# Program order at four output projections, three raw buffers in the first stage, and seven products of quarters in the first squared-ReLU MLP of a two-block fp32 transformer kernel

## Chip, cores and metric

The kernel runs on one core of one Trainium2 chip. The metric is the device time of one execution in microseconds. Three runs of the kernel before gave a median of 1999.02 us (1995.79 to 1999.51).

## What is computed

Two blocks of a transformer work on one sequence of 512 tokens with 1024 features, in fp32. The first block is a mixer (a forgetting attention and a chunked attention beside it), a cross attention to 256 memory rows, and a SwiGLU MLP. The second has an mLSTM layer and an MLA layer, each with an MLP of a squared ReLU behind it, and its norms are modulated by rows that are computed from a vector c. Cut to what this change touches:

```python
def rms_norm(x, g):                                   # over the 1024 features
    return x * lax.rsqrt(jnp.mean(x * x, -1, keepdims=True) + EPS) * g

def sqrelu_mlp(h, w1, w2):                            # w1: 1024x4096, w2: 4096x1024
    return jnp.square(jax.nn.relu(h @ w1)) @ w2

# first block
mix = concat([o_f, o_c]) @ w_out;   x = x + rms_norm(mix, g_mix_post)      # projection 1
ca  = attention_to_memory(...) @ w_mem_o;  x = x + rms_norm(ca, g_mem_post) # projection 2
x = x + rms_norm(swiglu(rms_norm(x, g_ffn_pre)), g_ffn_post)
# second block, for l in 0 (mLSTM), 1 (MLA)
ada = silu(c) @ ada_w[l] + ada_b[l];  sh1, sc1, g1, sh2, sc2, g2 = split(ada, 6)
y = mixer_l(modulate(rmsnorm(x), sh1, sc1)) @ w_out_l                       # projections 3 and 4
x = x + g1 * rmsnorm(y);  h = modulate(rmsnorm(x), sh2, sc2)
x = x + g2 * rmsnorm(sqrelu_mlp(h, w1[l], w2[l]))
```

## The kernel before

**Numbers in two parts.** Every operand of TensorE is kept as a rounded part `hi` and a rest `lo`. `prod` (L447, L448, L449) makes each product by three matmuls, hi·hi, hi·lo and lo·hi, on 128x512 or 128x256 outputs. ACT makes `hi` and DVE makes `lo = x - hi`: for activations in `parts` (L629, L630), for weights in `split` (L307 and L308, or L317 and L318 with a gain). Weights come by 512 KB DMAs on SP's queue into `raw` buffers, of which four may be live (`pump`), and `tick` deals out their splitting in pieces as TensorE's work is written down.

**What sets the order.** The program is written in one pass and a scheduler then orders the instructions of each engine by priority; inside an engine they run in that order, each waiting for what it needs. Work written under `hot` is moved ahead by 300 places. `ordered()` switches the scheduler off for PE, ACT, DVE and Pool within its block, so that they keep the order in which the code is written.

**Boundaries.** `boundary` closes a sublayer and opens the next. For each of the four token tiles t, `y_of(t)` makes the output of the tile (in `out_lin` the second half of its columns, 24 matmuls of 128x512, since the first half of all tiles stands ahead of it), `a(t)` adds the normed output to the stream x (mean of squares at L579, reciprocal root on POOL at L562 and L568, addition at L651), `scaled(t)` scales it for the next sublayer (L598), and `put(t)` transposes it by eight PE transposes (L609), modulates it in the second block (L616 on DVE, L619 on ACT) and splits it (L629, L630). The next sublayer's first products (`first`) need `put` of tiles 0 and 1 first. `out_lin` (L716) is the output projection and calls `boundary` with `fixed=True`: `put(t-2)` then stands four products into `y_of(t)` and `put` of the last tiles between the first units. With `fixed=False` these steps stand after `y_of(t)`. The four calls of `out_lin` are at L1215, L1898, L1920 and L1940; the last two modulate. `mlp` (L1344) also ends in `boundary`, with `fixed=True` for the SwiGLU MLP and the last MLP, which has no sublayer behind it (`nxt` is None), and `fixed=False` for the first squared-ReLU MLP.

**The two squared-ReLU MLPs.** `relu2` computes the 32 column blocks of `h @ w1` in 16 pairs, in five groups (6, 8, 6, 6, 6 blocks), with the down products of a group behind its up products. The first MLP has `h` of class `HT` and takes each pair by `relu_pairs`: 48 matmuls of 128x512. The second has `h` of class `HS`: after the first group (three pairs) each of the other 13 pairs is made by `wino` (L492): seven products of quarters (Strassen's scheme) with 84 matmuls of 128x256 (L510). That takes sums of weight quarters (`split7`, L331), sums of quarters of `h` (`quarters`, L473) and five 128x256 combinations of the results per pair (L524 to L534) on DVE.

**Background rows.** The modulation rows `ada` are computed by DVE from weights that POOL's queue loads (`row_by`: multiply-add at L873, DMA at L878, halves added at L882, then split at L630, one matmul with ones at L891, result read at L908). One step of this generator is written whenever TensorE's written work has passed 1.9 units of cost (`step_bg`). `y2` is the number of empty steps between the split of a half row and its matmul.

**The first stage.** `mixer1_values` starts as soon as x[0] and the first weights are there. `self.before` (L1087) names ahead of which weight load the DMAs of x[1], and of x[2] and x[3], go into SP's queue.

## Time and profile before

| | |
|---|---|
| median of three runs | 1999.02 us (1995.79 to 1999.51) |
| the profiled execution: its time, its span | 1995.13 us, 1993.3 us |
| mean granted clock of TensorE over the span | 0.991 |
| PE busy | 1941.7 us, 97% of the span |
| DVE busy | 1276.1 us, 64% |
| ACT busy | 1037.3 us, 52% |
| POOL busy | 351.5 us, 18% |
| chain of work that ended last, by engine | PE 90%, ACT 4%, DVE 4%, issue 1% |

The page has one execution; its own time lies 1.8 us above its span and 3.9 us under the median. A busy share is an average over stages, so the waits of PE and the windows of single stages say more than the share of an engine over the whole span.

### The profile page before, as it was taken

How to read it: one execution, taken by the hardware profiler on the slowest of the kernel's cores; microseconds unless marked ns; L12 is line 12 of the kernel's file. 1: busy time of each engine (PE TensorE's matmuls, PEld its weight loads, DVE VectorE, ACT ScalarE, POOL GpSimd, SP SyncE). 2: the span in 40 equal slices, each digit the busy share in tenths (PEclk: the TensorE clock that was granted, in tenths of full speed). 3: DMA queues.
4: the chain of work that ended last, by engine and by line, in shares of the span. 5: the costliest groups of instructions: out<-in, count | busy, mean ns of one | idle time of the engine just before them, and what ended most of it. 6: DMA issues, size and time to landing. Idle time of an engine off the chain costs nothing.

```text
span 1993.3 us, 28466 instructions
## 1 busy us (share of the span) xinstructions
PE 1941.7 (97%) x10222; PEld 1645.7 (83%) x10222; DVE 1276.1 (64%) x2517; ACT 1037.3 (52%) x2282; POOL 351.5 (18%) x703
## 2 busy tenths in 40 slices
PE   7999999998999999999998999999999999999998
PEld 5888987878888888878877888888888879989987
DVE  5756655765766785666885557654458655656765
ACT  6767775456334343455646442433566555545443
POOL 1331111211221231212232222210020012000000
PEclk9999999999999999999999999999999999999999
DMA  6332333442655563345462446533042121233222
GB/s 202 91 80 65 117 125 112 145 138 64 190 181 164 175 212 127 103 128 154 125 192 94 126 161 222 165 112 119 29 126 69 64 85 43 75 107 116 96 82 77
DMA packets 175246, 241.95 MB, mean 121 GB/s; under 512 B 20107, under 2 KB 117536, under 8 KB 175104
## 3 DMA queue, kind: packets, MB, share of 16 engines
q1 hardware_dynamic: 150704, 170.53, 27.1%
q0 software_dynamic: 24400, 69.60, 11.4%
q8 instruction: 80, 1.31, 0.3%
q14 instruction: 62, 0.51, 0.1%
HBM read 237.88 MB, written 2.20 MB: 120 GB/s over the span
## 4 chain that ended last, share of the span: by engine, by line
PE 90%; ACT 4%; DVE 4%; issue 1%; DMA 0%; POOL 0%; SPq 0%; DVEq 0%; POOLq 0%; ACTq 0%
PE ps L447 25%; PE ps L448 24%; PE ps L449 24%; PE ps L510 6%; PE ps L1033 1%; PE ps L609 1%; PE ps L1823 1%; ACT s L317 1%; PE ps L1852 1%; PE ps L1004 1%; PE ps L1583 1%; DVE s L318 1%; PE ps L1017 1%; PE ps L1320 1%; ACT junk L579 1%
## 5 line engine op out<-in xcount | busy, mean ns | idle before, releaser
L447 PE MATMUL ps<-s,s 128*128 128x512 f32 (+3 forms) x2468 | 940.2, 383 | 28.5 <-ACT s L629 28.5
L448 PE MATMUL ps<-s,s 128*128 128x512 f32 (+3 forms) x2468 | 928.3, 377 | 0.1
L449 PE MATMUL ps<-s,s 128*128 128x512 f32 (+3 forms) x2468 | 924.4, 377 | 2.0 <-DVE s L630 2.0
L447 PEld LDWEIGHTS ps<-s,s 128*128 128x128 f32 (+1 forms) x2468 | 467.2, 190 | 114.6 <-ACT s L629 31.5
L449 PEld LDWEIGHTS ps<-s,s 128*128 128x128 f32 (+1 forms) x2468 | 466.3, 189 | 91.3 <-DVE s L630 2.5
L448 PEld LDWEIGHTS ps<-s,s 128*128 128x128 f32 (+1 forms) x2468 | 467.3, 189 | 83.7 <-DVE s L630 1.0
L307 ACT ACTIVATE s<-raw 128x512 fp32r<-128x512 f32 x329 | 186.3, 623 | 177.3 <-PE ps L449 130.7
L308 DVE TENSOR_TENSOR s<-raw,s 128x512 fp32r<-128x512 f32 x329 | 213.9, 688 | 87.8 <-ACT s L307 85.9
L873 DVE SCALAR_TENSOR_TENSOR u<-araw,cond,u 128x512 f32<-128x512 f32 x224 | 168.5, 752 | 31.9 <-DMA araw<-in_ada_w 21.9
L317 ACT ACTIVATE s<-raw,cols_all 128x256 fp32r<-128x256 f32 (+1 forms) x305 | 142.7, 544 | 59.5 <-PE ps L449 25.2
L318 DVE SCALAR_TENSOR_TENSOR s<-raw,cols_all,s 128x256 fp32r<-128x256 f32 (+1 forms) x305 | 146.2, 538 | 30.8 <-ACT s L317 30.5
L878 POOL DMA_DIRECT2D araw<-in_ada_w x192 | 104.2, 543 | 283.2 <-DVE u L873 236.2
L630 DVE TENSOR_TENSOR s<-u,s 128x512 fp32r<-128x512 f32 x118 | 80.1, 689 | 115.1 <-ACT s L629 92.6
L510 PEld LDWEIGHTS ps<-s,s 128*128 128x128 f32 x1092 | 130.2, 188 | 1.0
L568 POOL TENSOR_SCALAR sm<-sm,sm 128x1 f32<-128x1 f32 x34 | 16.5, 485 | 647.8 <-ACT junk L579 519.8
L510 PE MATMUL ps<-s,s 128*128 128x256 f32 x1092 | 130.5, 280 | 0.0
L629 ACT ACTIVATE s<-u 128x512 fp32r<-128x512 f32 x118 | 72.2, 627 | 53.6 <-PE ps L449 27.0
L630 DVE TENSOR_TENSOR s<-ps,s 128x512 fp32r<-128x512 f32 (+3 forms) x100 | 59.5, 606 | 36.9 <-ACT s L629 35.8
L1465 ACT ACTIVATE u<-ps 128x512 f32<-128x512 f32 x38 | 22.6, 596 | 114.9 <-PE ps L449 111.0
L1368 DVE TENSOR_TENSOR u<-ps,u 128x512 f32<-128x512 f32 x80 | 54.3, 687 | 39.7 <-PE ps L449 39.6
L629 ACT ACTIVATE s<-ps 128x512 fp32r<-128x512 f32 (+3 forms) x100 | 51.2, 526 | 23.5 <-PE ps L609 10.2
L318 DVE SCALAR_TENSOR_TENSOR s<-raw,cols_mix,s 128x128 fp32r<-128x128 f32 (+2 forms) x152 | 52.4, 401 | 11.0 <-ACT s L317 10.6
(261 smaller groups left out, 2011.0 us busy)
## 6 DMA issues: line engine op xcount, KB each, us to landing
raw<-in_mlp_w SPq DMA_DIRECT2D x128, 512.0 KB, 3.8
araw<-in_ada_w POOLq DMA_DIRECT2D x192, 256.0 KB, 3.4
raw<-in_w_gate_up SPq DMA_DIRECT2D x44, 512.0 KB, 4.5
raw<-in_w_in SPq DMA_DIRECT2D x24, 512.0 KB, 4.1
raw<-in_a_w_in SPq DMA_DIRECT2D x24, 512.0 KB, 4.6
raw<-in_w_down SPq DMA_DIRECT2D x22, 512.0 KB, 3.8
raw<-in_w_mem_kv SPq DMA_DIRECT2D x16, 512.0 KB, 3.5
araw<-in_kv_ada_w POOLq DMA_DIRECT2D x32, 256.0 KB, 3.6
```

What stands on the lines that cost most here:

```text
L307: A.activation(hi[:, sl, cl], src[:, sl, cl], AF.Copy)
L308: f.tensor_tensor(out=lo[:, sl, cl], in0=src[:, sl, cl], in1=hi[:, sl, cl].bitcast(F32), op=ALU.subtract)
L317: A.activation(hi[:, i, :], src[:, i, :], AF.Copy, scale=g)
L318: V.scalar_tensor_tensor(out=lo[:, i, :], in0=src[:, i, :], scalar=g, in1=hi[:, i, :].bitcast(F32), op0=ALU.mult, op1=ALU.subtract)
L447: self.nc.tensor.matmul(ps, lhsT=ah, rhs=bh, start=first and i == 0, stop=False)
L448: self.nc.tensor.matmul(ps, lhsT=ah, rhs=bl, start=False, stop=False)
L449: self.nc.tensor.matmul(ps, lhsT=al, rhs=bh, start=False, stop=last and i == n - 1)
L510: nc.tensor.matmul(ps, lhsT=l[:, k, :], rhs=m[:, k, :], start=first and k == e == 0, stop=k == 3 and e == 2, skip_group_check=True)
L629: self.nc.scalar.activation(hi, x, AF.Copy)
L630: self.nc.vector.tensor_tensor(out=lo, in0=x, in1=hi.bitcast(F32), op=ALU.subtract)
L873: V.scalar_tensor_tensor(out=acc, in0=raws.pop(j), scalar=vec[:, j:j + 1], in1=acc, op0=ALU.mult, op1=ALU.add)
L878: nc.gpsimd.dma_start(out=raws[j], in_=ws[:, j, :])
```

## The change

1. The boundaries of the four output projections run in program order: `boundary(fixed=True)` is written inside `self.ordered()` and without `hot`.
2. All MLP boundaries now have `fixed=False`. That moves the one of the SwiGLU MLP (the last one has nothing behind it, and the first squared-ReLU MLP had it so).
3. In the first stage three `raw` buffers may be live and not four, and the loads of x[1] to x[3] each stand one weight load later in SP's queue.
4. The input of the first squared-ReLU MLP is an `HS` and not an `HT`, so that 13 of its 16 up pairs are made by seven products of quarters.
5. `y2` is 2 and not 1: one more background step lies between the split of a half row and its matmul.

```diff
-... y1=0, y2=1, y3=0, ...
+... y1=0, y2=2, y3=0, ...
@@ __init__
+        self.rcap = BUF["raw"] - 1
@@ pump
-                if self.raw_live + len(loaders) <= BUF["raw"]:
+                if self.raw_live + len(loaders) <= self.rcap:
@@ boundary
-        hot = lambda: self.hot("hb")
-        with nullcontext():
+        hot = nullcontext if fixed else lambda: self.hot("hb")
+        with self.ordered() if fixed else nullcontext():
             for t in range(NT):
@@ mixer1
-        self.before = {1: [lambda: get(1)], 3: [lambda: get(2), lambda: get(3)], 6: [biases]}
+        self.before = {2: [lambda: get(1)], 4: [lambda: get(2), lambda: get(3)], 6: [biases]}
...
             self.mixer1_values(h, vf, w)
+        self.rcap = BUF["raw"]
@@ mlp
-    def mlp(self, blocks, up, w_down, g, nxt, first, ready=None, caps=None, fixed=True):
+    def mlp(self, blocks, up, w_down, g, nxt, first, ready=None, caps=None):
...
-                self.boundary(y_of, nxt, first, fixed=fixed)
+                self.boundary(y_of, nxt, first, fixed=False)
@@ relu2
-        self.mlp(BUF['mb'], up, self.a["mlp_w2_2"][l], g, nxt, first, ready, BUF['mc'], fixed=nxt is None)
+        self.mlp(BUF['mb'], up, self.a["mlp_w2_2"][l], g, nxt, first, ready, BUF['mc'])
@@ the mLSTM layer's projection
-        hn = HT(self, KD)
+        hn = HS(self, KD)
         self.out_lin(a["a_w_out_2"][0], ho, g, nxt(4, 3, hn), self.relu_pairs(hn, a["mlp_w1_2"][0], 0, BUF["fp"], True), "head")
```

Lines of the changed kernel are one higher from L152 on and two higher from L1092 on.

**ACT at projection 1.** `s_802` and `s_804` are the halves of the next sublayer's input that `put(1)` fills, `s_818` to `s_823` weights of the cross attention, `x_10` the stream's token tile 2, `ps_3719` and `ps_3721` the output of tile 3. In the kernel before ACT has:

```order
L579 ACTIVATE junk_3713,sm_3712<-x_10_91 128x1024
L317 ACTIVATE s_818_3726<-raw_3510,cols_all_1926 128x256 x4
L317 ACTIVATE s_819_3735<-raw_3523,cols_all_1926 128x256 x4
L317 ACTIVATE s_822_3758<-raw_3540,cols_all_1926 128x256 x4
L317 ACTIVATE s_823_3767<-raw_3557,cols_all_1926 128x256 x4
L579 ACTIVATE junk_3773,sm_3772<-ps_3719 128x512
L629 ACTIVATE s_802_3677<-ps_3738 128x4x128
L629 ACTIVATE s_804_3681<-ps_3743 128x4x128
```

and in the changed one:

```order
L580 ACTIVATE junk_3715,sm_3714<-x_10_91 128x1024
L318 ACTIVATE s_818_3728<-raw_3510,cols_all_1926 128x256 x2
L630 ACTIVATE s_802_3679<-ps_3740 128x4x128
L630 ACTIVATE s_804_3683<-ps_3745 128x4x128
L318 ACTIVATE s_818_3728<-raw_3510,cols_all_1926 128x256 x2
L580 ACTIVATE junk_3775,sm_3774<-ps_3721 128x512
```

The two halves of `put(1)` stood behind 16 weight pieces and the mean of squares of tile 3, and now stand behind two weight pieces. On PE the transposes of `put(1)` moved with them, from the end of tile 3's 24 matmuls to their middle.

**ACT at projection 3.** `u_2022`, `u_2023` (before) and `u_1998`, `u_1999` (changed) are tile 1 on its way through the modulation, and `s_2015`, `s_2017` and `s_1993`, `s_1994` the halves of the MLP's input. Before:

```order
L307 ACTIVATE s_2031_10540<-raw_10259 128x512 x2
L307 ACTIVATE s_2032_10549<-raw_10266 128x512 x2
L307 ACTIVATE s_2036_10582<-raw_10348 128x512 x2
L307 ACTIVATE s_2037_10591<-raw_10363 128x512 x2
L579 ACTIVATE junk_10597,sm_10596<-ps_10533 128x512
L619 ACTIVATE u_2022_10516<-ps_10554,cols_1324_6645,cols_1385_7069 128x128 x2
L619 ACTIVATE u_2023_10518<-ps_10563,cols_1324_6645,cols_1385_7069 128x128 x2
L598 ACTIVATE u_2042_10601<-x_10_91,sm_10531 128x512
L598 ACTIVATE u_2043_10603<-x_10_91,sm_10531 128x512
L629 ACTIVATE s_2015_10491<-u_2022_10516 128x4x128
```

Changed:

```order
L580 ACTIVATE junk_10469,sm_10468<-x_10_91 128x1024
L308 ACTIVATE s_2007_10482<-raw_10215 128x512 x2
L620 ACTIVATE u_1998_10458<-ps_10496,cols_1330_6756,cols_1405_7233 128x128 x2
L620 ACTIVATE u_1999_10460<-ps_10505,cols_1330_6756,cols_1405_7233 128x128 x2
L630 ACTIVATE s_1993_10435<-u_1998_10458 128x4x128
L630 ACTIVATE s_1994_10438<-u_1999_10460 128x4x128
L308 ACTIVATE s_2008_10491<-raw_10222 128x512 x2
L580 ACTIVATE junk_10539,sm_10538<-ps_10475 128x512
```

Eight weight pieces, the mean of squares of tile 3 and the scaling of tile 2 stood ahead of the first half's split; now two weight pieces and the modulation itself stand there.

**DVE in the first squared-ReLU MLP.** `araw` are loaded rows of the modulation's weights. Before, around an up pair:

```order
L630 TENSOR_TENSOR s_2280_12229<-u_2278_12224,s_2280_12229 128x512
L873 SCALAR_TENSOR_TENSOR u_2265_12145<-araw_12187,cond_4169,u_2265_12145 128x512
L308 TENSOR_TENSOR s_2286_12271<-raw_12100,s_2286_12271 128x512 x2
L873 SCALAR_TENSOR_TENSOR u_2265_12145<-araw_12207,cond_4169,u_2265_12145 128x512
L308 TENSOR_TENSOR s_2290_12308<-raw_12125,s_2290_12308 128x512 x2
L873 SCALAR_TENSOR_TENSOR u_2265_12145<-araw_12209,cond_4169,u_2265_12145 128x512
L308 TENSOR_TENSOR s_2293_12341<-raw_12197,s_2293_12341 128x512 x2
L882 TENSOR_TENSOR u_2265_12145<-u_2265_12145 64x512
L630 TENSOR_TENSOR s_2280_12229<-u_2279_12225,s_2280_12229 128x512
```

Changed, around an up pair (L343 to L362 split and add quarters of the weights, L525 to L535 combine the products):

```order
L874 SCALAR_TENSOR_TENSOR u_2469_13725<-araw_13801,cond_4172,u_2469_13725 128x512
L525 TENSOR_TENSOR u_2491_13836<-ps_13777,u_2484_13793 128x256
L343 TENSOR_TENSOR s_2487_13811<-raw_13617,s_2487_13811 128x512
L874 SCALAR_TENSOR_TENSOR u_2469_13725<-araw_13803,cond_4172,u_2469_13725 128x512
L343 TENSOR_TENSOR s_2487_13811<-u_2488_13814,s_2487_13811 128x512
L527 TENSOR_TENSOR u_2492_13838<-ps_13776,u_2491_13836 128x256
L343 TENSOR_TENSOR s_2493_13852<-raw_13617,s_2493_13852 128x512
L631 TENSOR_TENSOR s_2477_13768<-u_2460_13630,s_2476_13767 128x512
L874 SCALAR_TENSOR_TENSOR u_2469_13725<-araw_13832,cond_4172,u_2469_13725 128x512
L346 TENSOR_TENSOR u_2488_13814<-u_2488_13814,raw_13617 128x512
L529 TENSOR_TENSOR u_2483_13780<-ps_13778,u_2492_13838 128x256
```

The background's multiply-adds now stand among combinations that wait for single products of PE (`ps`) and among the quarter sums of the weights that PE takes next.

## Rows read from the trace of the kernel before

**Rows 1.** The page, busy time of each engine, share of the span, instructions:
```profile
PE 1941.7 (97%) x10222; PEld 1645.7 (83%) x10222; DVE 1276.1 (64%) x2517; ACT 1037.3 (52%) x2282; POOL 351.5 (18%) x703
```

**Rows 2.** Waits of PE: line, releaser: us in total, times, longest us:
```profile
PE ps L447 <- ACT s L629: 28.5, 9, 6.1
...
PE ps L891 <- DVE u L630: 2.8, 1, 2.8
```

**Rows 3.** Windows: us, busy us (instructions) by engine, TensorE clock, DMA share, GB/s:
```profile
300.00:350.00 50.00, 45.09 (x223) 38.17 (x222) 26.41 (x52) 29.98 (x68) 9.02 (x20) 0.93 0.35 113
450.00:500.00 50.00, 44.92 (x298) 41.14 (x297) 29.00 (x56) 31.03 (x68) 8.16 (x19) 0.93 0.21 64
1050.00:1100.00 50.00, 43.87 (x257) 38.84 (x256) 27.32 (x50) 29.18 (x62) 11.31 (x20) 0.93 0.24 79
1600.00:1650.00 50.00, 45.14 (x231) 38.38 (x231) 26.27 (x47) 30.04 (x66) 12.14 (x18) 0.93 0.23 74
...
1110.00:1160.00 50.00, 50.00 (x217) 40.34 (x216) 25.71 (x39) 16.41 (x30) 13.30 (x25) 1.00 0.44 137
```

**Rows 4.** Timeline of all engines, projection 1: start us, us, instruction [idle before <-releaser]:
```profile
332.53 6.48 ACT L317 ACTIVATE s<-raw,cols_all 128x256 fp32r<-128x256 f32 x16
...
334.21 1.04 PE L609 MATMUL ps<-ident,u 128*128 128x128 f32 x8
...
338.91 0.57 ACT L579 ACTIVATE junk<-ps 128x512 bf16<-128x512 f32 x1
...
339.48 1.06 ACT L629 ACTIVATE s<-ps 128x512 fp32r<-128x512 f32 x2
...
340.11 0.80 PE L447 MATMUL ps<-s,s 128*128 128x256 f32 x2 [4.86 <-ACT s L629]
```

**Rows 5.** Timeline of ACT, then of DVE and PE, projection 3:
```profile
1074.15 4.26 ACT L307 ACTIVATE s<-raw 128x512 fp32r<-128x512 f32 x8
...
1078.88 1.48 ACT L619 ACTIVATE u<-ps,cols,cols 128x128 f32<-128x128 f32 x4
...
1081.47 0.63 ACT L629 ACTIVATE s<-u 128x512 fp32r<-128x512 f32 x1
...
1076.41 0.73 DVE L616 TENSOR_SCALAR u<-ps,cols,cols 128x128 f32<-128x128 f32 x2
1077.05 4.29 DVE L308 TENSOR_TENSOR s<-raw,s 128x512 fp32r<-128x512 f32 x7
...
1082.16 0.79 PE L447 MATMUL ps<-s,s 128*128 128x256 f32 x2 [6.13 <-ACT s L629]
```

**Rows 6.** Windows, columns as in Rows 3: first MLP, second MLP, a stretch of the mLSTM layer:
```profile
1095.00:1425.00 330.00, 330.00 (x1483) 269.73 (x1482) 180.92 (x277) 128.54 (x227) 56.20 (x106) 1.00 0.44 140
...
1650.00:1975.00 325.00, 325.00 (x2065) 293.52 (x2064) 208.11 (x361) 162.18 (x305) 9.94 (x10) 1.00 0.27 87
...
930.00:990.00 60.00, 60.00 (x339) 52.14 (x338) 52.65 (x103) 39.00 (x104) 20.66 (x35) 1.00 0.47 145
```

**Rows 7.** DVE's groups by form in 1095:1425: busy us, mean ns | idle before:
```profile
L873 DVE SCALAR_TENSOR_TENSOR u<-araw,cond,u 128x512 f32<-128x512 f32 x72 | 53.8, 748 | 13.1 <-DMA araw<-in_ada_w 9.5 <-DMA u<-in_ada_b 1.3 <-issue 1.1
...
L630 DVE TENSOR_TENSOR u<-u,u 64x512 fp32r<-64x512 f32 x10 | 6.9, 686 | 10.3 <-ACT u L629 10.1
L882 DVE TENSOR_TENSOR u<-u 64x512 f32<-64x512 f32 x9 | 6.2, 687 | 0.3
```

**Rows 8.** Groups by form in 1650:1975, of DVE and of PE:
```profile
L532 DVE SCALAR_TENSOR_TENSOR u<-ps,u 128x256 f32<-128x256 f32 x13 | 5.5, 422 | 14.1 <-PE ps L510 14.1
...
L510 PE MATMUL ps<-s,s 128*128 128x256 f32 x1092 | 130.5, 280 | 0.0
```

**Rows 9.** Timeline of PE, first stage and the end of the first MLP:
```profile
28.65 0.79 PE L447 MATMUL ps<-s,s 128*128 128x512 f32 x1 [3.30 <-ACT s L629]
...
1458.45 0.63 PE L449 MATMUL ps<-s,s 128*128 128x320 f32 x1 [1.97 <-DVE s L630]
```

**Rows 10.** Windows, columns as in Rows 3: after the waits at 892.62, 340.11 and 1458.45:
```profile
892.60:896.00 3.40, 3.38 (x15) 2.79 (x16) 1.65 (x3) 0.48 (x1) 1.29 (x3) 1.00 0.02 2
1458.40:1461.60 3.20, 3.15 (x12) 3.15 (x13) 2.53 (x14) 2.62 (x7) 1.27 (x4) 0.50 0.93 256
340.20:345.40 5.20, 5.15 (x23) 4.86 (x24) 5.20 (x12) 5.20 (x12) 0.42 (x1) 0.50 0.79 284
```

More of the change, by code (lines that the diff above doesn't have):

```diff
@@ L32 @@
 ALL = slice(0, S)
-BUF = dict(s8=14, u2=15, row=2, raw=4, w0=4, w1=4, w2=4, w3=5, w4=5, w5=5, w6=5, w7=5, ps=8, pace=1.9, pacb=1.9, man=0, lag=3, lagx=3, lagm=3, half=1, quiet=1, xp=0, fp=2, r1=1.25, r1b=3.6, r1c=2.4, r2=1.6, r2b=2.6, rx=1.4, rm=0.6, pre=10, gl=3, pl=0, hb=300, hs=0, ha=0, sp=0, spq=1.3, sq=1, b1=1, b2=1, lc=6, ar=4, mb=(6, 8, 6, 6, 6), mc=(4, 3, 4, 4, 4), st2=1, pr2=8, z1=4.5, z2=5, gt=3, rv=2, gs=1, rl=3, n1=4, ex=2, em=3, vg=1, sb=(8, 8, 6), mo=4, x1=2, g0=20, st=1, y1=0, y2=1, y3=0, ph=0, pq=0, fy=1, u1=6, s32=4, sm=60)
+BUF = dict(s8=14, u2=15, row=2, raw=4, w0=4, w1=4, w2=4, w3=5, w4=5, w5=5, w6=5, w7=5, ps=8, pace=1.9, pacb=1.9, man=0, lag=3, lagx=3, lagm=3, half=1, quiet=1, xp=0, fp=2, r1=1.25, r1b=3.6, r1c=2.4, r2=1.6, r2b=2.6, rx=1.4, rm=0.6, pre=10, gl=3, pl=0, hb=300, hs=0, ha=0, sp=0, spq=1.3, sq=1, b1=1, b2=1, lc=6, ar=4, mb=(6, 8, 6, 6, 6), mc=(4, 3, 4, 4, 4), st2=1, pr2=8, z1=4.5, z2=5, gt=3, rv=2, gs=1, rl=3, n1=4, ex=2, em=3, vg=1, sb=(8, 8, 6), mo=4, x1=2, g0=20, st=1, y1=0, y2=2, y3=0, ph=0, pq=0, fy=1, u1=6, s32=4, sm=60)
 TWO_PI = 2.0 * np.pi
```

## The prediction

> **What bounds the kernel now.** I read the page's busy times first: PE works 97% of the span [rows 1], so only two things can move the time: less work for PE, or less waiting of PE. Then the waits of PE, to see which releaser ends them: 28.5 us of all its idle time end at the split of activations on ACT, in nine waits of at most 6.1 us, and one wait of 2.8 us is the background rows' matmul with ones [rows 2]. Then windows of 50 us around the four output projections: PE is idle there for 4.91, 5.08, 6.13 and 4.86 us, 20.98 in all, and the granted clock is 0.93, while a window inside the first MLP has PE busy for all of 50.00 us at clock 1.00 [rows 3]. Last, the timeline of the first of them: the transposes of tile 1 end on PE at 335.25, but ACT goes from 332.53 to 339.01 through 16 weight pieces, takes the mean of squares of tile 3, and only at 339.48 splits what PE waits for; PE resumes at 340.11 [rows 4]. The data was there, and the order on ACT held it back. At projection 3 it is the same with eight larger pieces (4.26 us) on ACT and seven (4.29 us) on DVE [rows 5].
>
> **The clock belongs to these waits.** After the wait at 340.11 the next 5.2 us are granted 0.50, the 1.2 GHz level, and PE is busy for 5.15 of them: at full rate that is half, so 2.6 us are lost [rows 10]. All four windows show 0.93 [rows 3], so about 7 us at the low level each, partly idle. I take 2.6, 2.0, 2.0 and 2.6, since less of it falls on work where the wait is longer or starts later: 9.2. The four waits with their clock cost 20.98 + 9.2 = **30.2 us**.
>
> **Part 1, program order at the projections.** The changed order puts the transposes of tile 1 in the middle of tile 3's 24 matmuls, and its splits on ACT behind two weight pieces. A matmul of 128x512 takes 50.00/217 = 0.2305 us [rows 3], so 12 of them give 2.77 us of cover. At projections 1 and 2 there is to be done in it: two pieces (6.48/16 = 0.40 each), two splits (1.06) [rows 4] and the rest part on DVE (0.69, the length of the like group [rows 7]), 2.55 us together: covered, no wait left, at most some tenths. At projections 3 and 4 the modulation is in the chain: two pieces (4.26/8 = 0.53 each, 1.07), four scalings on ACT (1.48), a split (0.63) and the second one behind it (0.53) [rows 5], and the rest part (0.69): 4.4 us, so 4.4 - 2.77 = 1.6 us, say 1.7, stay at each. With 0.6 for small waits at all four the part gives 30.2 - 3.4 - 0.6 = **26 us**. Bounds: whether a wait of 1.7 us still lowers the clock. After the background's 2.8 us wait the clock is 1.00; after the two waits at the end of the first MLP, the second of 1.97 us [rows 9], it is 0.50 for 3.2 us [rows 10], which would cost 1.6 at each of two places. So 23 to 30. What is queued behind: the weight pieces that ACT and DVE now do later serve the next sublayer's later units; ACT is busy for 26 to 31 us of each 50 there and DVE for 26 to 29 [rows 3], so they have room, but the moved pieces are wanted some 10 us later, which is in the lower bound.
>
> **Part 2, the SwiGLU MLP's boundary.** It loses its fixed places: the order has the transposes of tile 2 only ten matmuls (2.3 us) ahead of their use, a unit of 24 (5.5 us) before. The chain there has the modulation too, up to 4.4 us from the terms above without waiting pieces 3.3. I charge **+0.5**, with 0 to +2.
>
> **Part 3, the first stage.** PE waits 3.30 us there for a split of tile data [rows 9]. Weights now arrive ahead of x[1], by one load of 512 KB; but in the order the split that PE waits for still stands behind the same weight pieces of ACT. **-0.5**, between -2.5 and +1.5, the width of that wait either way.
>
> **Part 5, one more background step.** The wait of the matmul with ones, 2.8 us [rows 2], comes from its split not being done one step after it is written. One step more is 1.9 units of TensorE's work, so it should go: **-2.8**. The row's chain gets a step longer, 11 and not 10 per half row, so that 11 half rows fall into the first MLP and not 10.
>
> **Part 4, seven products.** *PE.* A pair goes from 48 matmuls of 0.2305 (11.06 us) to 84 of 130.5/1092 = 0.1195 (10.04 us) [rows 3, 8]: 1.02 less, 13.3 for 13 pairs; the pair in the first group that is now made in halves costs +0.4. **-12.9** on PE. *DVE.* It pays for it. The second MLP has the seven products and no background rows: DVE is busy for 208.1 of 325 us and PE loses nothing; the first has background rows and no seven products: 180.9 of 330 [rows 6]. With both, DVE gets 208 and, for 11 half rows, 88 multiply-adds of 0.748, 11 splits of 0.686 and 11 additions of 0.687 (66 + 15 = 81 us) [rows 7]: 289 in some 317 us, a busy share of 0.91. The densest stretch of the trace without a loss of PE has 52.65 of 60, 0.88 [rows 6]. Busy times overlap: seven in a row take 4.29 us, which is (4.29 - 0.68)/6 = 0.60 from start to start [rows 5], 0.08 under the length of one. Counting the changed order's rows over the stage from the first products to the last pair (306 us for PE at the lower work): 314 of 128x512 at 0.60, 88 multiply-adds at 0.67 and 65 combinations of 128x256 at 0.422 - 0.08 = 0.34 [rows 7, 8]: 188 + 59 + 22 = 269 us. DVE has 37 us to spare, and of idle time that the background brings with it it had 13.1 us before the multiply-adds (mostly for DMA) and 10.3 before their splits [rows 7]. DVE takes its rows in order: where a combination waits for one of PE's products, the weight sums behind it wait too, and PE's next pair after them. Bounds: no stall, as in the second MLP (-12.9), and a stall for all of those 23.4 us (+10.5). The need (0.91) lies close above the row that shows no loss (0.88), so I take a third of 23.4, 8 us: **-5** for the part.
>
> The Trainium skill, Perfetto Trace Analysis, section "Identifying the Most-Contended Engine", holds that Vector's occupancy is a fair measure of how near that engine is to its limit. By that rule 0.91 is under PE's 1.00 and the whole 12.9 us would come, rival 1 below. The trace half agrees: the stretch at 0.88 shows no loss of PE [rows 6], but nothing in it is above that share.
>
> **Sum.** -26 + 0.5 - 0.5 - 2.8 - 5 = -33.8 us. The terms are from the profiled execution of 1995.13 us (span 1993.3), 3.9 us under the median; I take the difference off the median, as none of the terms depends on which run it was: 1999.0 - 33.8 = **1965 us**. Differences under 0.2%, 4 us, can't be told from no change in a measurement of this kernel.
>
> **Rivals.**
> 1. *All of it comes.* DVE's rows fit between PE's, as in the second MLP, and the projections leave no wait: -30 - 12.9 - 2.8 = -45.7, 1954 us. For: PE at 325.00 of 325 us in the second MLP [rows 6]. Against: the modulation's chain of 4.4 us against 2.77, and DVE at 0.91.
> 2. *DVE is the bound in the first MLP.* The background's idle times turn into PE's stalls in full: +10.5 and not -5, so 1980 us; PE then shows waits for DVE's L343 and L309 (the changed lines). For: a share that no stretch of the trace has. Against: the background's steps are not urgent, and PE's own rows have slack of several buffers.
> 3. *Program order does not remove the waits.* If PE stops in the middle of tile 3 for transposes whose input (additions and scaling of tile 1) is late, the wait only moves, and the clock with it: 20 of the 26 us stay, 1985 us. For: in program order nothing else can fill PE. Against: the scaling of tile 1 ends well before that point in the trace: even its transposes are done at 335.25, 4.9 us before PE needs them [rows 4].
> 4. *Slower than before.* The same DVE mechanism as in 2, but DVE is held up far more often, since it takes rows in strict order, and background rows wait for DMA in front of PE's weights. The place is the 306 us of the first MLP, the price all of the 34 us and more, and it decides where DVE's occupied share there falls under 269/(306 + 42) = 0.77: then this stage takes 348 us and not 306, which with -29 from the rest gives +0 or more against before; at 0.75 it is 359 us, and the kernel 2010 us. The mLSTM stretch reaches 0.88 busy, some 0.8 occupied, without waiting [rows 6], so this needs a worse pattern than any seen.
>
> **Chances.** The forecast 0.46, rival 1 0.18, rival 2 0.20, rival 3 0.11, rival 4 0.05. The forecast's own range, with the bounds of parts 1 to 3 and half of part 4's, is 1957 to 1975. The range for 8 in 10 reaches into rivals 1 and 2 in full and to rival 3's own time: 1950 to 1985; left out are rival 4, the upper half of 3 and the far end of 1. Rivals 1 to 3 are all faster than before by over 0.2%; so faster is 0.93, rival 4 gives 0.05 slower, and 0.02 lies between.
>
> **What would show it.** In the changed profile the four windows at the projections should have PE busy for 48 us or more of 50 and the clock at 1.00 at the first two; a row of waits "L448 <- ACT L630" of a few us in place of 28.5. The wait of the ones' matmul should be gone. In the first MLP PE's gaps should sum to about 8 us, ended by DVE's weight sums; none means rival 1, 23 means rival 2, over 40 rival 4. Wrong would make it: waits of 3 us and more in the middle of tile 3 at the projections, DVE under 0.77 occupied while PE waits for it, or a new wait at the SwiGLU MLP's end of over 2 us.

## The result and the profile after

The changed kernel takes 1982.78 us (median of six runs, 1981.07 to 1986.34) against 1998.97 us before (six runs, 1995.79 to 1999.51): a ratio of 0.9923, 95% interval 0.9910 to 0.9936, or 16 us less. The prediction had 1965 us, 34 us less, and a range of 1950 to 1985. The sign and the range held; the gain was 16 us of the 34.

The page of the changed kernel, head and busy times (share of the span, instructions):

```profile
span 1981.0 us, 29787 instructions
## 1 busy us (share of the span) xinstructions
PE 1929.0 (97%) x10738; PEld 1658.4 (84%) x10738; DVE 1373.0 (69%) x2689; ACT 1067.2 (54%) x2355; POOL 361.1 (18%) x711
```

PE's busy time fell by 12.7 us against [rows 1], about the work that the seven products were to save (12.9), and its idle time is 52.0 us for 51.6. So PE waits as long as before, in other places. Its waits in the changed kernel (line, releaser: us in total, times, longest us):

```profile
PE ps L448 <- ACT s L630: 15.3, 10, 3.9
PE ps L892 <- DVE u L631: 6.1, 4, 4.7
PE ps L511 <- DVE u L527: 5.8, 3, 5.4
PE ps L387 <- DMA u<-in_g_mix_pre: 5.0, 1, 5.0
PE ps L610 <- DVE u L1625: 3.1, 1, 3.1
PE ps L449 <- DVE s L631: 2.1, 5, 0.8
PE ps L450 <- DVE s L631: 1.9, 1, 1.9
```

The 28.5 us of [rows 2] are down to 15.3. New are the second row, the background's matmul with ones, and the third, a product of the seven that waits for DVE's combination of earlier products. Windows at the four projections and over the first squared-ReLU MLP (us, busy us of PE, PEld, DVE, ACT and POOL, TensorE clock, DMA share, GB/s):

```profile
300.00:350.00 50.00, 48.65 (x266) 41.05 (x265) 23.75 (x51) 26.66 (x60) 9.04 (x20) 1.00 0.26 79
450.00:500.00 50.00, 48.66 (x318) 43.51 (x317) 32.05 (x61) 30.12 (x66) 8.20 (x19) 1.00 0.29 87
1040.00:1090.00 50.00, 46.63 (x279) 41.16 (x278) 27.58 (x51) 29.01 (x62) 8.51 (x19) 0.97 0.18 58
1582.00:1632.00 50.00, 46.60 (x234) 38.83 (x233) 25.66 (x47) 27.62 (x62) 5.14 (x13) 0.98 0.17 53
1095.00:1425.00 330.00, 317.52 (x1937) 282.27 (x1936) 286.65 (x471) 160.69 (x304) 79.94 (x140) 0.98 0.48 152
```

Against [rows 3], projections 1 and 2 lost their long wait and their slow clock; projections 3 and 4 keep 3.4 us of idle time each and half of the slow clock. In the MLP, PE was busy for all of 330 us before [rows 6] and now idles for 12.5, with DVE busy for 287 us (289 in 317 were forecast); over 9 us of these are one blocked instruction, shown below.

Where the time went, by the starts of the same PE instructions in the two timelines:

| until | before, us | after, us | after less before | this stretch |
|---|---|---|---|---|
| wait in the mixer, behind the first stage | 224.85 | 225.78 | +0.9 | +0.9 |
| wait in the cross attention, behind projection 1 | 430.37 | 426.33 | -4.0 | -5.0 |
| PE resumes at projection 2 | 471.41 | 463.78 | -7.6 | -3.6 |
| PE stops at the end of the mLSTM layer | 1037.84 | 1025.27 | -12.6 | -4.9 |
| PE resumes at projection 3 | 1082.16 | 1069.11 | -13.1 | -0.5 |
| PE stops at the end of the first squared-ReLU MLP | 1455.15 | 1445.15 | -10.0 | +3.1 |
| PE resumes at projection 4 | 1640.65 | 1629.61 | -11.0 | -1.0 |
| end | 1993.33 | 1981.03 | -12.3 | -1.3 |

The spans differ by 12.3 us and the medians by 16.2. The profiled execution of before (1995.13 us) is one of its fastest, that of after (1982.94) lies at its median; the 3.9 us between can't be put into a stage.

### The profile page after: what moved, and what is told of

Its sections match the earlier page's. It is cut to its first block, busy times and chain, and to the rows that moved or that the text cites. A ratio compares the mean times of both kernels' runs of the same rounds, so it can differ in the third digit from the quotient of the medians.

```text
span 1981.0 us, 29787 instructions
## 1 busy us (share of the span) xinstructions
PE 1929.0 (97%) x10738; PEld 1658.4 (84%) x10738; DVE 1373.0 (69%) x2689; ACT 1067.2 (54%) x2355; POOL 361.1 (18%) x711
## 3 DMA queue, kind: packets, MB, share of 16 engines
q0 software_dynamic: 24400, 69.60, 11.4%
## 5 line engine op out<-in xcount | busy, mean ns | idle before, releaser
L448 PE MATMUL ps<-s,s 128*128 128x512 f32 (+4 forms) x2276 | 858.3, 380 | 15.4 <-ACT s L630 15.3
L449 PE MATMUL ps<-s,s 128*128 128x512 f32 (+4 forms) x2276 | 848.2, 374 | 2.1 <-DVE s L631 2.1
L450 PE MATMUL ps<-s,s 128*128 128x512 f32 (+4 forms) x2276 | 843.3, 374 | 1.9 <-DVE s L631 1.9
L448 PEld LDWEIGHTS ps<-s,s 128*128 128x128 f32 (+2 forms) x2276 | 430.1, 189 | 92.1 <-ACT s L630 19.3
L450 PEld LDWEIGHTS ps<-s,s 128*128 128x128 f32 (+2 forms) x2276 | 430.0, 189 | 81.1 <-DVE s L631 3.0
L449 PEld LDWEIGHTS ps<-s,s 128*128 128x128 f32 (+2 forms) x2276 | 430.9, 189 | 76.8 <-DVE s L631 3.2
L511 PE MATMUL ps<-s,s 128*128 128x256 f32 x2184 | 263.5, 281 | 6.2 <-DVE u L527 5.8
L511 PEld LDWEIGHTS ps<-s,s 128*128 128x128 f32 x2184 | 261.7, 189 | 9.3 <-ACT u L531 5.6
L308 ACT ACTIVATE s<-raw 128x512 fp32r<-128x512 f32 x277 | 158.0, 623 | 149.2 <-PE ps L450 96.7
L309 DVE TENSOR_TENSOR s<-raw,s 128x512 fp32r<-128x512 f32 x277 | 187.7, 716 | 62.2 <-ACT s L308 61.0
L631 DVE TENSOR_TENSOR s<-u,s 128x512 fp32r<-128x512 f32 x126 | 84.9, 686 | 60.2 <-ACT s L630 40.3
L569 POOL TENSOR_SCALAR sm<-sm,sm 128x1 f32<-128x1 f32 x34 | 12.7, 375 | 581.9 <-ACT junk L580 454.2
L630 ACT ACTIVATE s<-u 128x512 fp32r<-128x512 f32 x126 | 76.4, 625 | 59.9 <-DVE u L1432 24.6
L342 ACT ACTIVATE s<-raw 128x512 fp32r<-128x512 f32 x104 | 62.5, 621 | 72.6 <-PE ps L450 37.9
L631 DVE TENSOR_TENSOR s<-ps,s 128x512 fp32r<-128x512 f32 (+3 forms) x100 | 59.1, 606 | 37.1 <-ACT s L630 29.7
L343 DVE TENSOR_TENSOR s<-raw,s 128x512 fp32r<-128x512 f32 x104 | 70.5, 682 | 12.2 <-ACT s L342 11.9
L342 ACT ACTIVATE s<-u 128x512 fp32r<-128x512 f32 x78 | 48.5, 623 | 53.1 <-DVE u L346 30.2
```

The costliest lines, as they stand in the source:

```text
L308: A.activation(hi[:, sl, cl], src[:, sl, cl], AF.Copy)
L309: f.tensor_tensor(out=lo[:, sl, cl], in0=src[:, sl, cl], in1=hi[:, sl, cl].bitcast(F32), op=ALU.subtract)
L342: A.activation(hi, x, AF.Copy)
L448: self.nc.tensor.matmul(ps, lhsT=ah, rhs=bh, start=first and i == 0, stop=False)
L449: self.nc.tensor.matmul(ps, lhsT=ah, rhs=bl, start=False, stop=False)
L450: self.nc.tensor.matmul(ps, lhsT=al, rhs=bh, start=False, stop=last and i == n - 1)
```

## Experiments

The kernel before was timed anew beside each set of runs, with medians of 1998.97 to 2000.36 us. So a difference between kernels of two sets is good to about 1.4 us.

### One part alone, one part undone

Three kernels split the change: program order at the four projections alone in the kernel before, the seven products alone in it, and the changed kernel without the seven products.

```diff
# order_only (kernel before)
-        hot = lambda: self.hot("hb")
-        with nullcontext():
+        hot = nullcontext if rows else lambda: self.hot("hb")
+        with self.ordered() if rows else nullcontext():
...
-        self.boundary(y_of, nxt, first, late)
+        self.boundary(y_of, nxt, first, late, rows=True)
# seven_only (kernel before); no_seven is the same line turned round in the changed kernel
-        hn = HT(self, KD)
+        hn = HS(self, KD)
```

> The kernel before with program order at the four output projections alone. By the stages of the two traces (theory A) this edit by itself saves about 17 us (20.9 us of waiting falls to about 9.5, and of 9 us of slow clock some 3 stay), so 1982 us, as much as the whole change: then all other edits together are worth nothing. By the prediction's sum (theory B) it saves 26 us, 1973 us, and another edit costs what is missing.

> The kernel before with the seven products in the first squared-ReLU MLP alone. Theory A (the stage's trace: PE does 12.9 us less there but waits some 12 us more and loses some 5 us to the clock) expects 1999 to 2006 us, no gain. Theory B (a gain of 5 us, hidden in the whole by other losses) expects 1994 us. If the new waits come from the mix with program order or the later background step, the seven products alone give up to 12.9 us, 1986.

> The changed kernel without the seven products. Theory A expects 1977 to 1983 us (the seven products cost some 3 us or are worth nothing); theory B expects 1988 us. Here too: if it is 1995, the seven products work and everything else fails.

Program order alone: 1987.66 us against 2000.09, ratio 0.9936 (0.9922 to 0.9951), 12 us less, where theory A expected 17 and theory B 26. In this kernel projection 3 keeps waits of 0.59 and 4.10 us with 6.8 us of slow clock, and two waits that the kernel before has at full clock (2.77 us, here at 883.54, and 2.16 us, here at 1032.13) have 3.4 us of slow clock each. The seven products alone: 2006.58 us, ratio 1.0030 (1.0017 to 1.0043), **slower** by 6.5 us. The change without the seven products: 1981.05 us, not distinguishable from the change with them. So in the changed kernel the seven products brought nothing, and theory B is wrong on them. The waits of PE with the seven products alone:

```profile
PE ps L447 <- ACT s L629: 28.1, 10, 5.0
PE ps L891 <- DVE u L630: 7.6, 2, 4.9
...
PE ps L510 <- ACT u L530: 4.4, 1, 4.4
PE ps L386 <- DMA u<-arow: 3.6, 1, 3.6
```

Beside the projections' old row stand new ones of 3.6 to 4.9 us, at the ones' matmul, at the modulation's columns (`arow`) and inside the seven products.

### Weight pieces behind the splits at the projections

At projection 3 the changed kernel's timeline shows why 3 us are left. ACT first, then DVE, then PE (start us, us, instruction, idle time and its releaser):

```profile
1063.27 1.06 ACT L580 ACTIVATE junk<-x 128x1024 bf16<-128x1024 f32 x1 [1.36 <-DVE x L652]
...
1064.33 1.14 ACT L308 ACTIVATE s<-raw 128x512 fp32r<-128x512 f32 x2
1067.03 1.50 ACT L620 ACTIVATE u<-ps,cols,cols 128x128 f32<-128x128 f32 x4 [1.56 <-DVE u L617]
1068.41 1.16 ACT L630 ACTIVATE s<-u 128x512 fp32r<-128x512 f32 x2
...
1064.98 1.29 DVE L309 TENSOR_TENSOR s<-raw,s 128x512 fp32r<-128x512 f32 x2 [1.80 <-ACT s L308]
1066.19 1.36 DVE L617 TENSOR_SCALAR u<-ps,cols,cols 128x128 f32<-128x128 f32 x4
...
1069.11 0.38 PE L448 MATMUL ps<-s,s 128*128 128x256 f32 x1 [3.02 <-ACT s L630]
```

PE's transposes of tile 1 are done at 1063.29. But ACT takes the mean of squares of tile 2 and two weight pieces (L308), and DVE, whose two rest parts (L309) stand ahead of the modulation (L617), waits 1.80 us for these. The modulation on ACT (L620) waits for that on DVE. The experiment writes the two pieces behind the splits:

```diff
                 g, n = y_of(t), 0
+                if nxt and t >= 2 and fixed:
+                    self.credit = -4 * 0.65
...
                         self.put(*pend.pop(t - 2))
+                        for _ in range(2):
+                            if self.pieces:
+                                self.piece()
```

> The changed kernel, with the two weight pieces of each of the last two token tiles of a projection written behind the transposes and splits of the next input and not ahead of them. If the wait of 3 us left at projections 3 and 4 is made by these two pieces (ACT splits them, DVE waits for that before it may modulate), it falls to 1 us or less and the slow clock behind it goes: 4 us at each, 1975 us. If it is the chain of the modulation itself, nothing or 1 us is gained at each, 1981 to 1983 us.

1977.06 us, ratio 0.9884 (0.9867 to 0.9900): 5.7 us under the changed kernel. DVE and ACT at projection 3:

```profile
1060.49 1.36 DVE L617 TENSOR_SCALAR u<-ps,cols,cols 128x128 f32<-128x128 f32 x4
...
1060.67 1.06 ACT L580 ACTIVATE junk<-x 128x1024 bf16<-128x1024 f32 x1 [1.37 <-DVE x L652]
...
1061.73 1.49 ACT L620 ACTIVATE u<-ps,cols,cols 128x128 f32<-128x128 f32 x4
1063.10 1.15 ACT L630 ACTIVATE s<-u 128x512 fp32r<-128x512 f32 x2
```

DVE modulates at once, ACT right behind the mean of squares, and PE waits 0.33 and 0.34 us (at 1063.79 and 1064.52) in place of 3.02 and 0.34, with no slow clock behind. The two pieces made the wait. The gain is less than the 4 us at each of projections 3 and 4, since the MLP behind takes 1.4 us more (377.5 us from PE's resuming to its stop for 376.0): the ones' matmul there waits 6.09 us, with 10.2 us of slow clock.

### Quarter additions on DVE and not on POOL

The largest new wait in the first MLP stands at 1119.94. DVE, then POOL, then PE around it, in the changed kernel:

```profile
1109.73 10.06 DVE L631 TENSOR_TENSOR u<-u,u 64x384 fp32r<-64x384 f32 x1 [0.59 <-ACT u L630]
...
1109.40 9.97 POOL L483 TENSOR_TENSOR u<-s 128x512 f32<-128x512 f32 x8
...
1119.94 0.66 PE L892 MATMUL ps<-u,onesr 128*128 128x384 f32 x1 [4.65 <-DVE u L631]
```

One DVE instruction on half a tile takes 10.06 us, and ends 0.4 us after POOL's eight additions (the sums of hi and lo in `quarters`). The clock is at 0.50 from inside this wait on, and from inside the second large wait, which ends at 1396.88, too:

```profile
1117.84:1124.60 6.76, 4.66 (x11) 3.79 (x12) 6.63 (x9) 0.34 (x1) 3.02 (x5) 0.50 0.02 3
1394.40:1401.00 6.60, 4.12 (x16) 3.87 (x17) 5.56 (x10) 1.87 (x5) 0.51 (x1) 0.50 0.74 235
```

```diff
-                G.tensor_tensor(out=x, in0=hi[:, k].bitcast(F32), in1=lo[:, k].bitcast(F32), op=ALU.add)
+                V.tensor_tensor(out=x, in0=hi[:, k].bitcast(F32), in1=lo[:, k].bitcast(F32), op=ALU.add)
```

> The changed kernel with the eight additions of hi and lo in quarters written for DVE and not for POOL. Theory C: at 1109 us one DVE instruction on 64x384 takes 10 us, as long as eight POOL additions of 128x512 run back to back, because the two engines can't read two SBUF operands at the same time; PE then waits 4.7 us for it and loses 2.4 us more to the clock. If so, the 10 us instruction and the wait go, DVE gets 8 x 0.6 = 4.8 us of work, and the time falls by 4 to 7 us, to 1976 to 1979. Rival: the DVE instruction waits for something else (a buffer, PE), then the wait stays and the time is 1983 to 1987.

1976.16 us, ratio 0.9888 (0.9869 to 0.9908): 6.6 us less, though DVE has eight instructions more in each of the two MLPs. No DVE instruction of that stage is long any more, and the ones' matmul is gone from that stage's waits (one of 0.89 us is left in the mLSTM layer, at 893.52):

```profile
PE ps L448 <- ACT s L630: 15.8, 11, 3.9
PE ps L511 <- DVE u L527: 5.4, 1, 5.4
PE ps L387 <- DMA u<-in_g_mix_pre: 4.6, 1, 4.6
PE ps L610 <- DVE u L1625: 3.1, 1, 3.1
```

From PE's resuming at projection 3 to its stop at the end of the MLP it is 1069.14 to 1437.16, 368.0 us; the kernel before takes 373.0 (1082.16 to 1455.15) and the changed one 376.0. Theory C holds: without POOL's additions the stage takes 8.0 us less, and the seven products gain 5.0 us in it.

The same block, of 10.01 to 10.93 us, stands in all eight kernels with the seven products in this MLP and POOL's additions. In the one with these products alone DVE's row and POOL's are

```profile
1126.02 10.63 DVE L345 TENSOR_TENSOR u<-raw,raw 128x512 f32<-128x512 f32 x1
...
1126.12 9.97 POOL L482 TENSOR_TENSOR u<-s 128x512 f32<-128x512 f32 x8
```

where 0.69 us is usual for DVE's. The Trainium skill, SBUF — State Buffer, section "Who interferes with whom", says that a DVE instruction with two inputs in SBUF contends with a GpSimd instruction that reads SBUF, and that the second to issue waits until the first has finished. The trace agrees as to the kind of instructions, but here DVE waited for all eight in a row and not for one. And in this kernel, as in three others of the eight, DVE's record starts 0.10 to 0.25 us ahead of the first addition's, so by the records the one that started first was the one that waited.

### Is DVE too full? Two kernels that thin out the background

The second large wait, 5.39 us at 1396.88, lies in the last group of up pairs. DVE around it in the changed kernel:

```profile
1390.86 1.89 DVE L309 TENSOR_TENSOR s<-raw,s 128x512 fp32r<-128x512 f32 x3
1392.67 0.41 DVE L525 TENSOR_TENSOR u<-ps,u 128x256 f32<-128x256 f32 x1
1393.00 1.28 DVE L309 TENSOR_TENSOR s<-raw,s 128x512 fp32r<-128x512 f32 x2
1394.31 0.69 DVE L883 TENSOR_TENSOR u<-u 64x512 f32<-64x512 f32 x1
1395.10 0.69 DVE L343 TENSOR_TENSOR s<-u,s 128x512 fp32r<-128x512 f32 x1
1395.71 0.68 DVE L631 TENSOR_TENSOR s<-u,s 128x512 fp32r<-128x512 f32 x1
1396.31 0.42 DVE L527 TENSOR_TENSOR u<-ps,u 128x256 f32<-128x256 f32 x1
```

PE waits for L527, the second combination, and between the first (L525) and it stand five rows for later work, 3.3 us, with hardly a gap. The prediction had a stall by DVE's order too, but the other way round: weight sums behind a combination that waits, and not a combination behind rows for later work. It came as one wait of 5.4 us with its clock and not as many small ones.

```diff
# few_rows (changed kernel): background multiply-adds left out
+                elif j >= 0 and self.late and j % 4:
+                    raws.pop(j)
# behind_and_dve: the two edits above together
# rows_spread: behind_and_dve with
-pacb=1.9
+pacb=3.0
```

> The changed kernel, leaving out six of eight multiply-adds of the background's modulation rows from the third projection on (the second block's later modulation is wrong thereby); their DMAs stay. Theory D: the wait of 5.4 us at 1397 and the smaller ones in the first MLP come from DVE being full there. If so, all of PE's waits in that MLP but the one at 1115 to 1120 go, and the time falls by 8 to 10 us, to about 1973. Rival: the waits come from the order of DVE's rows alone, whatever they take; then the wait at 1397 stays at over 3 us, 1979 or more.

> The two edits together: weight pieces behind the splits at the projections, and the additions of the quarters on DVE. If they are independent, the gains add: 1977 less 4 to 7 us, 1970 to 1973.

> The same two edits, and the background rows from the third projection on are stepped every 3.0 and not every 1.9 units of PE's work, so that a third of them moves from the first MLP into the MLA layer. By theory D the wait at 1397 shrinks or goes: 4 to 7 us less than the run with two edits, 1964 to 1969. If the MLA layer's own chains are hit by the rows, it gives that back.

Without six of eight multiply-adds the wait at 1397 is gone: the window 1375 to 1440 has PE busy for 64.56 of 65 us.

```profile
1375.00:1440.00 65.00, 64.56 (x402) 57.84 (x401) 50.87 (x91) 41.99 (x85) 8.46 (x16) 1.00 0.34 104
```

But the time stayed at 1983.04 us, since other waits grew: 7.62 us at the end of the mLSTM layer (1033.84, 3.10 in the changed kernel), and 4.03 us at 1177.92 in the MLP. Leaving out instructions gave the scheduler another order everywhere, so this run bears on the wait's cause and not on its price, and theory D's number fell.

The two edits together: **1967.88 us**, ratio 0.9850 (0.9826 to 0.9874), 14.9 us under the changed kernel where the single runs give 5.7 + 6.6 = 12.3. By the ratios to the kernel before, each within its own set, it is 14.6 against 7.8 + 7.0, so the two gains add. It beats both kernels. Spreading the background: 1971.10 us, not told from the two edits alone. The wait at 1397 is gone here too, but the rows that moved delay the MLA layer and projection 4: new waits of 1.96 us at 1594.65 (for modulation columns), 1.96 at 1609.89 and 2.35 at 1628.27, the last with 6.8 us of slow clock. The wait at 1397 went in both kernels with fewer background rows there, so these rows make it (more on this with the background steps below); but what it cost came back elsewhere.

### The small parts undone

```diff
# first_as_before (changed kernel)
-        self.rcap = BUF["raw"] - 1
+        self.rcap = BUF["raw"]
-        self.before = {2: [lambda: get(1)], 4: ...
+        self.before = {1: [lambda: get(1)], 3: ...
# y2_one (changed kernel)
-y2=2
+y2=1
# swiglu_fixed (changed kernel): the SwiGLU MLP's boundary with fixed=True and the scheduler
# behind_no_seven: behind_and_dve with
-        hn = HS(self, KD)
+        hn = HT(self, KD)
```

> The changed kernel with the first stage as before (four raw buffers, loads of x one place earlier in the queue). The traces put PE 0.8 us later at the end of the first wait (29.47 for 28.65), so theory A expects 1 us less, 1981 to 1982; the prediction's -0.5 for the edit expects 1983 to 1984. The difference is near what a measurement can tell, so the trace's place of that wait decides.

> The changed kernel with one background step fewer before the ones' matmul, as before. The prediction's term is -2.8 us and the trace shows the wait at 892 fall from 2.77 to 0.38 us, so 1985 to 1986 us if nothing else hangs on it. But the waits of the same matmul in the first MLP (4.7, 0.9 and 0.2 us) should then grow too; and if the wait of 3.1 us at the end of the mLSTM layer (2.2 before) comes from this edit, it goes back to 2.2 us.

> The changed kernel with the SwiGLU MLP's boundary as before (fixed places, scheduler). The prediction's +0.5 for this edit and the new wait of 0.73 us at 851 in the trace expect 0.5 to 1 us less, 1982; if the wait of 3.1 us at the end of the mLSTM layer comes from this edit it goes back to 2.2 us too.

> The run with weight pieces behind the splits and quarter additions on DVE, with the first squared-ReLU MLP by plain products again. It says whether the seven products are worth anything once the contention and the projections' waits are gone. Theory A: PE's 12.9 us less against waits of some 8 us and 4 us of clock left in that MLP, so 1970 to 1973, 2 to 5 us more than with them (1968). If the plain products win, below 1967.

The first stage as before: 1981.09 us; its wait starts PE at 29.78 us in the run's own time, where the changed kernel has 29.47, and lasts 3.30 us and not 3.92. But the start's other waits scatter by 1 us between runs of like kernels, so this part is not told from nothing. The SwiGLU boundary as before: 1982.11 us; the wait of 0.73 us at 851 is gone, and the rest is as it was. The two small parts are as small as forecast.

The background step is the surprise: **1998.05 us** (ten runs), ratio 0.9994 to the kernel before. Undoing this one number takes away the gain but for 1 or 2 us, and the interval (0.9983 to 1.0005) doesn't tell these from nothing. PE's waits:

```profile
PE ps L448 <- ACT s L630: 15.9, 9, 3.9
PE ps L892 <- DVE u L631: 10.1, 3, 6.6
PE ps L387 <- DMA u<-arow: 5.9, 1, 5.9
...
PE ps L511 <- ACT u L531: 4.4, 1, 4.4
PE ps L610 <- DVE u L1625: 2.2, 1, 2.2
```

The wait at the end of the mLSTM layer goes back to 2.2 us, so 0.9 us there are this part's; 3.4 us of slow clock stand there in this kernel too. But in the first MLP the ones' matmul waits 6.6 us behind POOL's additions (with a slow clock of 10.2 us), the modulation's columns 5.9 us and a product of the seven 4.4 us, each of the last two with 6.8 us of slow clock: from projection 3 to the MLP's end it takes 386.8 us (1071.20 to 1457.98) and not 376.0. Without the seven products the step is worth less: program order alone takes 1987.66 us and the changed kernel without these products 1981.05, 6.6 apart, and these two differ by this part and the two small ones.

With both edits but without the seven products: 1978.18 us. Against 1967.88 the products are worth 10 us once the contention is gone, more than theory A gave (2 to 5). Part of this is the order again: this kernel has a wait of 3.20 us at 1087.76, between the first up products, that the one with `HS` has not, and 6.8 us of slow clock with it. Its MLP takes 377.9 us from PE's resuming to its stop, that of the changed kernel without the products 374.2, and the one with both edits 366.3: in these single executions the products gain 8 us there without that order.

### More background steps, and a last version

```diff
# y2_four (changed kernel)
-y2=2
+y2=4
# two_edits_undone: behind_and_dve, first stage and SwiGLU boundary as before
# two_edits_undone_y4: the same with y2=4
```

> The changed kernel with four background steps and not two between the split of a half row and its matmul with ones. If PE's wait at 1120 hangs on this matmul (the split is stuck behind POOL's additions and the matmul stands ahead of PE's other work), it goes with its clock, 7 us less: 1976. If DVE's weight sums are what PE needs then, the wait stays at over 3 us, with L511 for the waiting line: 1980 to 1983.

> The run with weight pieces behind the splits and quarter additions on DVE (1968), with the first stage and the SwiGLU MLP's boundary as in the kernel before. By the traces of the single runs each is worth 0.7 to 1.5 us: 1965 to 1967. If other waits take it up, 1968.

> The run before this one, with four background steps ahead of the ones' matmul. Without the contention the waits for that matmul are 0.5 to 1.4 us, so 1 to 2 us less than the run before this one, 1964 to 1966; if the later matmul delays the rows that the modulation needs, more.

Four steps in the changed kernel: 1979.09 us. DVE is blocked by POOL as long as before,

```profile
1101.30 10.75 DVE L631 TENSOR_TENSOR s<-u,s 128x512 fp32r<-128x512 f32 x1 [0.80 <-ACT s L630]
```

and PE does not wait there at all: the ones' matmuls next to it stand at 1080.47 and 1122.16. So PE's wait hung on the place of the ones' matmul in PE's order. The MLP takes 362.5 us (1063.92 to 1426.44), 13.5 less than in the changed kernel, and 5.2 us are gained ahead of it; of these 18.7 us 13.9 are given back, at projection 4 (3.69 and 1.83 us of waiting, with 10 us of slow clock) and in the MLA layer, whose modulation rows now come later.

The wait at 1397 is gone here too. The stretch from 70 to 20 us before PE's stop, in the changed kernel and in this one:

```profile
1375.15:1425.15 50.00, 44.61 (x266) 39.85 (x265) 36.00 (x62) 27.23 (x54) 6.39 (x12) 0.93 0.34 105
...
1356.44:1406.44 50.00, 50.00 (x328) 45.51 (x327) 37.48 (x67) 30.21 (x59) 3.42 (x8) 1.00 0.33 104
```

DVE is busier in the second, with no wait of PE. What differs is the background: eight of its multiply-adds lie in the first stretch and none in the second. Over all 13 kernels with the seven products in this MLP, the seven that have 7 or 8 multiply-adds in this stretch have the wait, of 5.4 to 5.5 us, and the six with none to two don't; in the two of these with `y2=1` a like wait of 4.4 us stands one group earlier, where their last half row ends. So which rows stand ahead of the combination makes the wait, and not DVE's busy share.

The last two: 1967.95 us (ratio 0.9840, 0.9825 to 0.9855) and 1966.27 us (0.9834, 0.9817 to 0.9852; 1964.09 to 1970.70). Neither is told from the two edits alone. The small parts don't add up to anything that these runs can show.

## Why the prediction was wrong

**Part 1, program order: the mechanism held, the size did not.** From the table and the waits, the four projections gained 4.7, 5.5, 3.1 and about 3 us with their clock, 16 and not 26. At projections 1 and 2 small waits of 0.49, 0.52 and 0.34 us were left at the transposes and at the two parts of the split, 1.3 at each, where 0.6 had been set down for all four. At 3 and 4 the term "1.7 us stay at each" measured 3.4. Its chain of 4.4 us left out three things that stand in the timeline after, in part at the same time: the mean of squares on ACT ahead of the pieces (1.06 us), DVE's wait for ACT's two pieces before it may modulate (1.80), and that ACT's half of the modulation starts behind DVE's half. And the clock fell at both (3.4 us at 0.50 each, 1.7 us of loss), which the text had as the bound and not as the value. The gain lay below the lower bound of 23.

**Part 4, seven products: the work was right, a cause was missing.** PE's work fell by 12.7 us and DVE's fill came out at 287 us for 289, though over 9 of these are the blocked instruction. The 8 us of stalls set down for it are about there: without POOL's additions PE waits 7.4 us in that MLP, 5.4 of them at one place with some 2 us of clock behind, and the MLP gains 5.0 us. That this is the forecast to the tenth is luck: the stall stood at another row than the text had, and 5.0 is the difference of two single executions. What was missing is that `quarters` puts eight additions on POOL while DVE has rows to do: 8.0 us. In the kernel before, the second MLP has the same additions, but there is no background in it, and its PE loses nothing [rows 6]. The prediction took the additions on POOL for free, and gave no reason why they would be hidden.

**Part 5, one more step: right as a wait, wrong in scope.** The wait at 892 fell from 2.77 to 0.38 us, as said, and 2.6 us came back at the end of the mLSTM layer: 0.9 of wait, and 1.7 of clock, which the changed kernel with one step has there too. But the 2.8 us were read off one wait in a kernel whose first MLP had slack. With the seven products in it the same number is worth 15 us, 10.7 of them in that MLP. There the ones' matmul stands in PE's order ahead of work that PE could do, and is held behind POOL's additions (6.6 us and its clock); why the waits of 5.9 and 4.4 us come with it is not shown.

**Parts 2 and 3** came as +0.7 (forecast +0.5) and +0.9 (-0.5, with a bound of +1.5) by the timelines; the runs that undo them tell neither from nothing. Together the stages give -16.3 + 0.7 + 0.9 + 0.2 + 3.1 = -11.4 us, of the 12.3 by which the spans differ. Against the forecast 9.7 us are missing at the projections, 8.1 in the first MLP and 3.0 in part 5.

**The rivals.** Rival 2 had the right place (the first MLP, +10.5 forecast, +3.1 measured) but the wrong cause in the main: a block of DVE by POOL, at one point, and not background rows all over; these made the wait at 1397, 5.4 of 12.4 us. Nor did PE's long gaps end at the weight sums that the prediction had named as its sign, L343 and L309. That its 1980 us lie near the measured time is luck, as its projections are 10 us too good; so is rival 3's 1985, since of its waits in the middle of tile 3 only 0.5 us came, at projections 1 and 2. Rival 4 did not come. Rival 1 was too high; as the prediction read the Trainium skill's rule on occupancy (Perfetto Trace Analysis, "Identifying the Most-Contended Engine"), PE would have lost nothing with DVE at 0.87 busy (286.65 of 330 us). It lost 12.5 us: this share shows neither the order of DVE's rows nor the neighbour that blocked it, and it counts the blocked time as busy.

**What stays open.** Why DVE is passed over for all eight additions in the first MLP, while at projection 4 of the changed kernel the two engines seem to take turns (of four weight pieces from 1636.15 on, 4.70 us together, two take 1.8 us beside additions of 1.5 and 1.7); and what the order of the first pairs, some 4 us of the 10 that the products are worth with both edits, hangs on.

## To carry to other kernels

Where DVE and POOL read SBUF at the same time, look for one instruction that lasts as long as a row of the other's. Here its cause was the neighbour, and the cure was to move the work to one side, though to the busier engine. A background instruction on the bounding engine waits for its own chain with everything behind it; give it more distance than its present wait asks for. A chain that is to fit into a cover has to be laid out row by row on every engine that it crosses, with what stands ahead of each row, and not as a sum of durations.

## What the runs showed of the hardware

DVE instructions with two SBUF inputs took 10.01 to 10.93 us in place of 0.6 to 0.7 while POOL ran eight additions of about 1.25 us back to back, in eight kernels and on two lines of the program (the splits' rest, L631, and the weights' quarter sums, L346 or L345). With four background steps one more takes 7.35 us in the second MLP, at 1661.37, behind six additions. And the fall of the clock is not set by the wait alone: after the wait of 3.10 us at the end of the mLSTM layer it was 0.50 for 3.4 us in the changed kernel and 1.00 in the one without the seven products, where the same wait, of the same length, stands at 1028.70:

```profile
1030.00:1033.00 3.00, 3.00 (x15) 2.43 (x14) 1.05 (x2) 0.00 (x0) 0.00 (x0) 1.00 0.42 128
```

So too the ones' matmul's wait of 2.77 us in the mLSTM layer: 1.00 behind it in the kernel before [rows 10], and 0.50 for 3.4 us with program order alone. Each such place is worth 1.7 us either way in one execution.
